# A hybrid convolution and gated-delta layer on one core: raw tokens in the first products, the fifth and sixth products tile by tile, the last product in pieces

## The chip, the cores and the metric

The kernel runs on one core of a Trainium2 chip. The metric is the device time of one execution in microseconds (us); lower is better. Before the change the median of three runs is 1960.46 us (1956.25 to 1960.53).

## The reference, cut to what matters

1024 tokens of width 1024, all in float32. Three residual stages, each behind an RMS norm:

```python
h = h + 0.5 * swiglu_ffn(rmsnorm(h, ffn1_norm), w1_in, w1_out)     # 1024 -> 2*2816 -> 1024
u = rmsnorm(h, mix_norm) @ w_mix_in                                # gates, convolution, q, k, v
h = h + concat([short_conv(u), gated_delta(u)]) @ w_mix_out
h = h + 0.5 * swiglu_ffn(rmsnorm(h, ffn2_norm), w2_in, w2_out)
return rmsnorm(h, final_norm)
# rmsnorm(x, w) = x * rsqrt(mean(x*x) + 1e-6) * w
```

## The kernel before, in words

The tokens lie transposed: eight tiles (d = 0 to 7) of 128 features by 512 tokens for each half of the tokens, `h[0]` and `h[1]`. Every float32 operand of a large product is split into a rounded part `hi` (ScalarE, L102) and the rest `lo` (VectorE, L103), and a product of two tiles is three matmuls (`mm3`, L190 to L194: hi·hi, lo·hi, hi·lo). Weights come through SyncE's queue into eight `raw` tiles (L95) and are split into seven pairs `whi`, `wlo`.

The products are saved by a Winograd form of Strassen's scheme: a `Pair` (L321) takes two column tiles of the weights and needs seven products of four `mm3` each instead of eight. The token blocks are A11, A12 (the first half, split in `split1`), S1, nS2, S3, S4 and A22 (`Blocks.sums`, L294, in three parts); the weight blocks are B11, B21, B22 and the sums T1 to T4, which GpSimd makes (`pool_tt`, L110). The head of a pair is product 1 (A11·B11, copied out of PSUM as `p1`, L351) and product 2 (added into the same bank, then `first`, L435). The body is products 6 (nS2·T2), 5 (S1·T1), 7, 4 and 3 (L364 to L407). Product 7 is added into the bank of product 6, L389 reads it, and product 4 goes on in the same bank.

At the start (`first_heads`, L607) the heads of five pairs run before the bodies. SyncE's queue fetches eight tiles of tokens by rows (`xtok`) for the norm's sums, then four token tiles and four weight tiles in turn. ScalarE squares the rows, GpSimd takes the power (L219), TensorE spreads the factor over the partitions (`spread`, L239, into the bank `rb`), VectorE scales each token tile by gain and factor (`norm1`, L281), and only then can a tile be split and used. The second half of the tokens follows the same way (`norms[1]`), and its `spread` releases `sums(0)`. `all_pairs` (L409) writes out the bodies of pairs 0 and 1 in turn: both sixth products, `sums(1)`, both fifth, `sums(2)`, both seventh, and so on. The same function is used by the first feed-forward stage, by the projection to q, k, v and by the second feed-forward stage.

`ffn_out` (L496) is the product with the second weight matrix: seven products of eleven steps (k = 0 to 10), each step four `mm3` (d = 0 to 3), one bank for each d. After the fifth (S1·T1) `t1_done` squares the first half and calls `after(26, 4)` (in the second feed-forward stage `after(30, 4)`): 26 `mm3` later TensorE sums the squares (`reduce`, L221), four later it spreads the factor. The weight sum T4 of the last product (A22·T4) is made on GpSimd, in its queue behind the norm's power. At the very end `reduce`, `spread` and `scale_out` run for the second half of the tokens with 512 columns at once.

A planner (`run_tasks`, L119) writes the code out: each task has a load, a preparation and a run; preparations are written four tasks ahead of the runs, loads nine. Tile's scheduler then orders instructions on an engine by the program order, except where one is ready earlier by its own model; `keep_in_program_order` forbids that. An engine runs its queue in order.

Of the kernel before, what the change touches and what calls it, by code (L numbers as in the profile page):

```python
# [56 lines left out]
def tile_hybrid(  # L57
# [145 lines left out]
    class Norm:  # L203
# [25 lines left out]
        def by_tokens(self, src):  # L229

            tot = const.tile([P, 8], F32, name="tot", tag="tot", bufs=2)
            for i, tile_ in enumerate(src):
                nc.scalar.activation(out=tile_, in_=tile_, func=AF.Square, accum_out=tot[:, i:i + 1])
# [33 lines left out]
    class Blocks:  # L267
# [3 lines left out]
        def __init__(self, h, which):  # L271
            self.h, self.g = h, V_N[which]
            self.s4 = []
            self.b = {n: [None] * KH for n in ("A11", "A12", "S1", "nS2", "S3", "S4", "A22")}
# [11 lines left out]

        def begin2(self, k):

            h2 = self.h[1]
            nc.scalar.activation(out=h2[k], in_=h2[k], func=AF.Copy, scale=self.gain(k))  # L290
# [3 lines left out]
        def sums(self, part, rb):  # L294

            h, b = self.h, self.b
            if part == 0:
                for k in range(KH):
                    s1, s2 = h[1][k], h[0][k]
                    nc.vector.tensor_tensor(out=s1, in0=s1, in1=rb, op=ALU.mult)  # L300
                    nc.vector.tensor_tensor(out=s2, in0=s2, in1=s1, op=ALU.subtract)  # L301
                    b["nS2"][k] = split(s2, slot)
                for k in range(KH):
                    b["S1"][k] = split(h[1][k], slot)
            if part == 1:
                for k in range(KH):
                    a22, s2 = h[1][k + KH], h[0][k]
# [13 lines left out]
    class Pair:  # L321
# [5 lines left out]
        def __init__(self, x, srcs, first, done):  # L327
            self.x, self.srcs, self.first, self.done = x, srcs, first, done
            self.r, self.t, self.w = {}, {}, {}
# [14 lines left out]
        def run_p1(self):  # L344
            self.x_ps = psum()
            prod(self.x_ps, self.w.pop("B11"), self.x.b["A11"], True)
            self.copy_p1()

        def copy_p1(self):
            self.p1 = temp4(F32, "p1")  # L350
            nc.scalar.copy(out=self.p1[:, 3:HALF + 3], in_=self.x_ps)  # L351

        def run_p2(self):
            prod(self.x_ps, self.w.pop("B21"), self.x.b["A12"], False)
            self.done("C11", self.first(self.x_ps))
# [5 lines left out]
        def head2(self):  # L361
            return self.run_p2, lambda: self.ready("B21"), lambda: self.get("B21")

# [45 lines left out]
    def all_pairs(pairs, x, norm2, between={}):  # L409
# [3 lines left out]
        for a in (0, 2):  # L413
            for n, two in enumerate(zip(*(p.body() for p in pairs[a:a + 2]))):
                if a == 0 and n in (1, 2):
                    task(None, lambda n=n: norm2.then(lambda: x.sums(n, norm2.rb)))
                for t in two:
                    task(*t)
# [11 lines left out]
    def gate_pair(x, w_in, j, gs, store):  # L430
        t = {}

        def first(ps):
            c = temp4(F32, "c11")
            nc.scalar.activation(out=c[:, 3:HALF + 3], in_=ps, func=AF.Silu)  # L435
# [18 lines left out]
    def ffn_in(x, norms, w_in, name, start=None):  # L454
# [31 lines left out]
        all_pairs(pairs, x, norms[1])  # L486
# [9 lines left out]
    def ffn_out(acc, fill, g_dr, w_out, t1_done, t2_done):  # L496
# [8 lines left out]
        def step(banks, a, b, k, start):  # L505
# [27 lines left out]
            def run():  # L533
                x, w = ops["x"], ops["w"]
# [934 lines left out]
```

## Time and profile before

| | |
|---|---|
| runs | 1956.25, 1960.46, 1960.53 us |
| profiled execution | 1959.77 us, of it 1958.0 us span |
| TensorE busy | 1833.8 us, 94% of the span |
| VectorE, ScalarE, GpSimd busy | 68%, 38%, 37% |
| mean granted TensorE clock | 0.971 |

A busy TensorE is not TensorE at its peak, since matmuls overlap in the records. In a stretch without waits 442 matmuls take 100 us. So a stretch is read by its count of matmuls against its length.

### The profile page before, as it was taken

What the parts mean: (1) busy time and instruction counts of PE and PEld (TensorE: products, weight loads), DVE (VectorE), ACT (ScalarE), POOL (GpSimd) and SP (SyncE); (2) the same over time, 40 slices, a digit from 0 to 9 for tenths busy, and PEclk for the clock granted to TensorE, in tenths of its full rate; (3) what the DMA queues carried; (4) which work ended last, traced back from release to release, by engine and by line L of the source; (5) the groups of instructions that cost most, each with busy time, mean ns of one, the idle gap of its engine ahead of it and who ended that gap; (6) DMA issues with size and microseconds to landing.
All of it is one profiled execution on the core that took longest, in us unless ns stands there. A gap on an engine that the chain in (4) does not pass through costs nothing.

```text
span 1958.0 us, 25016 instructions
## 1 busy us (share of the span) xinstructions
PE 1833.8 (94%) x8512; PEld 1493.6 (76%) x8512; DVE 1338.5 (68%) x1991; ACT 750.0 (38%) x1517; POOL 733.3 (37%) x510
## 2 busy tenths in 40 slices
PE   5799999999999899987799989998999999999996
PEld 4578888888888777676678877776888888888884
DVE  4876666567865797776974356688666566677655
ACT  6422323223544453377332243452323222344433
POOL 1464455355331434145311001036454355435142
PEclk9899999999999999998999979998999999999998
DMA  7144343437883423477742176423343434487532
GB/s 281 33 161 128 118 140 127 140 108 257 311 270 113 140 97 102 141 245 252 222 135 80 61 263 183 164 92 102 127 139 127 140 109 160 150 292 274 193 108 97
DMA packets 194512, 312.45 MB, mean 160 GB/s; under 512 B 27856, under 2 KB 48336, under 8 KB 194384
## 3 DMA queue, kind: packets, MB, share of 16 engines
q1 hardware_dynamic: 191216, 305.28, 47.0%
q10 hardware_dynamic: 3168, 5.57, 0.9%
q8 instruction: 67, 1.10, 0.2%
q14 instruction: 61, 0.50, 0.1%
HBM read 228.44 MB, written 82.33 MB: 159 GB/s over the span
## 4 chain that ended last, share of the span: by engine, by line
PE 74%; DVE 13%; issue 4%; DMA 3%; POOL 3%; ACT 3%; SPq 0%; POOLq 0%; DVEq 0%; ACTq 0%
PE ps_ps L192 20%; PE ps_ps L191 20%; PE ps_ps L193 20%; PE ps_mm L191 3%; PE ps_mm L192 3%; PE ps_mm L193 3%; DVE wlo L103 3%; PE ps_aux L862 1%; DVE lo L103 1%; DVE xb L1034 1%; DVE sv L1030 1%; DVE cv L774 1%; POOL T L110 1%; DMA raw<-w_in 1%; DVE h L301 1%
## 5 line engine op out<-in xcount | busy, mean ns | idle before, releaser
L191 PE MATMUL ps_ps<-hi,whi 128*128 128x512 f32 x1400 | 554.1, 396 | 23.0 <-DVE c L389 11.4
L193 PE MATMUL ps_ps<-hi,wlo 128*128 128x512 f32 x1400 | 552.7, 395 | 13.0 <-DVE wlo L103 12.9
L192 PE MATMUL ps_ps<-lo,whi 128*128 128x512 f32 x1400 | 553.0, 395 | 5.3 <-DVE lo L103 5.2
L103 DVE TENSOR_TENSOR wlo<-raw,whi 128x512 fp32r<-128x512 f32 x280 | 267.3, 964 | 119.4 <-ACT whi L102 118.4
L103 DVE TENSOR_TENSOR wlo<-T,whi 128x512 fp32r<-128x512 f32 x244 | 235.3, 978 | 144.5 <-ACT whi L102 142.4
L191 PEld LDWEIGHTS ps_ps<-hi,whi 128*128 128x128 f32 x1400 | 266.8, 191 | 85.4 <-issue 12.3
L193 PEld LDWEIGHTS ps_ps<-hi,wlo 128*128 128x128 f32 x1400 | 267.3, 191 | 71.7 <-DVE wlo L103 16.0
L192 PEld LDWEIGHTS ps_ps<-lo,whi 128*128 128x128 f32 x1400 | 266.9, 191 | 63.1 <-DVE lo L103 8.0
L110 POOL TENSOR_TENSOR T<-raw 128x512 f32<-128x512 f32 x144 | 224.6, 1561 | 232.3 <-DMA raw<-w_out 91.5
L191 PE MATMUL ps_ps<-ghi,whi 128*128 128x512 f32 x616 | 241.8, 393 | 7.2 <-ACT whi L102 7.2
L192 PE MATMUL ps_ps<-glo,whi 128*128 128x512 f32 x616 | 241.9, 393 | 1.4 <-DVE glo L103 1.4
L193 PE MATMUL ps_ps<-ghi,wlo 128*128 128x512 f32 x616 | 241.7, 393 | 1.2 <-DVE wlo L103 1.2
L102 ACT CAST whi<-raw 128x512 fp32r<-128x512 f32 x280 | 170.2, 617 | 86.1 <-PE ps_mm L192 19.1
L102 ACT CAST whi<-T 128x512 fp32r<-128x512 f32 x244 | 146.4, 617 | 81.4 <-POOL T L110 44.8
L191 PE MATMUL ps_mm<-hi,whi 128*128 128x512 f32 x384 | 158.0, 412 | 0.9 <-DVE u L400 0.9
L192 PE MATMUL ps_mm<-lo,whi 128*128 128x512 f32 x384 | 155.2, 404 | 1.2 <-DVE lo L103 1.2
L193 PE MATMUL ps_mm<-hi,wlo 128*128 128x512 f32 x384 | 154.2, 402 | 1.4 <-DVE wlo L103 1.4
L103 DVE TENSOR_TENSOR glo<-raw,ghi 128x512 fp32r<-128x512 f32 x154 | 128.9, 838 | 38.8 <-ACT ghi L102 37.2
L191 PEld LDWEIGHTS ps_ps<-ghi,whi 128*128 128x128 f32 x616 | 116.3, 189 | 33.6 <-ACT whi L102 8.4
L193 PEld LDWEIGHTS ps_ps<-ghi,wlo 128*128 128x128 f32 x616 | 116.3, 189 | 28.0 <-DVE wlo L103 2.7
L192 PEld LDWEIGHTS ps_ps<-glo,whi 128*128 128x128 f32 x616 | 116.4, 189 | 27.3 <-DVE glo L103 2.1
L110 POOL TENSOR_TENSOR T<-raw,T 128x512 f32<-128x512 f32 x50 | 73.3, 1465 | 167.2 <-DMA raw<-w_in 129.3
(226 smaller groups left out, 2286.5 us busy)
## 6 DMA issues: line engine op xcount, KB each, us to landing
raw<-w_in SPq DMA_DIRECT2D x264, 256.0 KB, 4.6
raw<-w_out SPq DMA_DIRECT2D x154, 256.0 KB, 4.3
raw<-w_qkv SPq DMA_DIRECT2D x36, 256.0 KB, 3.4
f1S<-S SPq DMA_DIRECT2D x33, 256.0 KB, 5.0
raw<-f1A SPq DMA_DIRECT2D x33, 256.0 KB, 3.9
raw<-f1S SPq DMA_DIRECT2D x33, 256.0 KB, 3.7
f2S<-S SPq DMA_DIRECT2D x33, 256.0 KB, 5.0
raw<-f2A SPq DMA_DIRECT2D x33, 256.0 KB, 4.5
```

The source lines that it names most:

```text
L102: tc.keep_in_program_order(nc.scalar.copy(out=hi, in_=src))
L103: nc.vector.tensor_tensor(out=lo, in0=src, in1=hi.bitcast(F32), op=ALU.subtract)
L110: tc.keep_in_program_order(nc.gpsimd.tensor_tensor(out=out, in0=in0, in1=in1, op=op))
L191: nc.tensor.matmul(out=ps, lhsT=whi, rhs=xhi, start=start, stop=False, skip_group_check=True)
L192: nc.tensor.matmul(out=ps, lhsT=whi, rhs=xlo, start=False, stop=False, skip_group_check=True)
L193: nc.tensor.matmul(out=ps, lhsT=wlo, rhs=xhi, start=False, stop=stop, skip_group_check=True)
L301: nc.vector.tensor_tensor(out=s2, in0=s2, in1=s1, op=ALU.subtract)
L774: nc.vector.scalar_tensor_tensor(out=acc, in0=u[:, i:i + HALF], scalar=vcol(wc + i), in1=acc, op0=ALU.mult, op1=ALU.add)
L862: nc.tensor.matmul(out=ps[:, sl], lhsT=lhs[:, sl], rhs=rhs[:, sl], start=start, stop=stop)
L1030: nc.vector.tensor_tensor(out=tv, in0=lrow[:, lo:hi].unsqueeze(2).broadcast_to([nb, n, j + 1]), in1=xrow[:, 0:j + 1].unsqueeze(1).broadcas ...
L1034: nc.vector.tensor_tensor(out=xv, in0=xv, in1=tv, op=ALU.subtract)
```

## The change

- Start: the first token tiles are fetched ahead of the rows. `split_raw` splits gain times token, without the norm's factor, and the first and second products of the five early pairs run on that. The factor (`rbs`) is put in by VectorE on leaving PSUM, in `copy_p1` and in `first`. The fifth pair's weights and all five B21 are fetched ahead of the second half's rows. `norm1` of the eight tiles still runs for the sums, and A11 and A12 are split once more, from the normed tokens, for the pairs from the sixth on (one tile every three `mm3`, after the bodies of pairs 0 and 1). One token tile lies in a `raw` tile.
- `sums(0)` splits S1 and nS2 block by block. `all_pairs` prepares T1 and T2 of pairs 0 and 1 first, then runs `both(k)`: for one block k the fifth and sixth products of both pairs; then `sums(1)`, the seventh products, `sums(2)`, and the rest. This holds for all three users of `all_pairs`.
- `after(26, 4)` and `after(30, 4)` become `after(14, 4)`.
- The small weights `wba` are loaded and split in a task after the first `ffn_out`, no longer wherever the scheduler puts them.
- Last product of the second `ffn_out`: steps k = 0 to 6 as before; steps 7 to 10 are held and run for one d after the other, with the add behind each. The closing norm's sum, power, spread, scaling and stores go in two halves of 256 columns. The ScalarE queue stores d = 1, 4 and 7.

```diff
+        def split_raw(self, d):
+            src = self.h[0][d]
+            hi, lo = slot(F32R, "hi"), slot(F32R, "lo")
+            tc.keep_in_program_order(nc.scalar.activation(out=hi, in_=src, func=AF.Copy, scale=self.gain(d)))
+            nc.vector.scalar_tensor_tensor(out=lo, in0=src, scalar=self.gain(d), in1=hi.bitcast(F32),
+                                           op0=ALU.mult, op1=ALU.subtract)
...
                 for k in range(KH):
-                    s1, s2 = h[1][k], h[0][k]
+                    s1 = h[1][k]
+                    s2 = self.s2[k] = slot(F32, "s2") if self.raw else h[0][k]
                     nc.vector.tensor_tensor(out=s1, in0=s1, in1=rb, op=ALU.mult)
-                    nc.vector.tensor_tensor(out=s2, in0=s2, in1=s1, op=ALU.subtract)
+                    nc.vector.tensor_tensor(out=s2, in0=h[0][k], in1=s1, op=ALU.subtract)
+                    b["S1"][k] = split(s1, slot)
                     b["nS2"][k] = split(s2, slot)
-                for k in range(KH):
-                    b["S1"][k] = split(h[1][k], slot)
...
         def copy_p1(self):
             self.p1 = temp4(F32, "p1")
-            nc.scalar.copy(out=self.p1[:, 3:HALF + 3], in_=self.x_ps)
+            if self.factor is not None:
+                nc.vector.tensor_tensor(out=self.p1[:, 3:HALF + 3], in0=self.x_ps, in1=self.factor, op=ALU.mult)
+            else:
+                nc.scalar.copy(out=self.p1[:, 3:HALF + 3], in_=self.x_ps)
...
+        def both(self, k):
+            if k == 0:
+                self.z, self.y = psum(), psum()
+            ks = slice(k * P, (k + 1) * P)
+            for ps, t, s in ((self.z, "T1", "S1"), (self.y, "T2", "nS2")):
+                w = self.w[t]
+                mm3(ps, w[0][:, ks], w[1][:, ks], *self.x.b[s][k], k == 0, k == KH - 1)
...
+                for one, two in zip(*products[:2]):
+                    task(None, one[1], one[2])
+                    task(None, two[1])
+                for k in range(KH):
+                    task(lambda k=k: [p.both(k) for p in pairs[:2]])
...
+            task(*head(early[4], 0))
+            task(lambda: [norms[0].spread(), scaled(), then()], lambda: [x.split_raw(d) for d in range(KH, KT)])
+            task(*head(early[0], 1))
+            task(*head(early[1], 1))
+            task(*head(early[2], 1))
+            task(*head(early[3], 1))
+            task(norms[1].spread)
+            task(*head(early[4], 1))
...
+                      {0: lambda: [later(3 * d, lambda d=d: x.split1(d)) for d in range(KT)]})
...
-            nm[0].after(26, 4)
+            nm[0].after(14, 4)
...
-            task(add)
+            if not by_tile:
+                task(add)
+                return
+            for d in range(KH):
+                task(lambda d=d: [one(d, i == KH - 1) for i, one in enumerate(held)] and add([d]))
...
+        for i in range(2):
+            two = slice(2 * i, 2 * i + 2)
+            for b in range(2 * i, 2 * i + 2):
+                nc.tensor.matmul(out=sums[:, b:b + 1], lhsT=last[1].acc[:, b * P:(b + 1) * P], rhs=ones[:, 0:1],
+                                 start=True, stop=True)
+            nc.vector.tensor_scalar(out=ms[:, two], in0=sums[:, two], scalar1=1.0 / D, scalar2=EPS,
+                                    op0=ALU.mult, op1=ALU.add)
+            nc.gpsimd.tensor_tensor(out=rs[:, two], in0=ms[:, two], in1=pneg[:, two], op=ALU.pow)
+        for i in range(2):
+            for b in range(2 * i, 2 * i + 2):
+                nc.tensor.matmul(out=last[1].rb[:, b * P:(b + 1) * P], lhsT=rs[:, b:b + 1].broadcast_to([P, P]),
+                                 rhs=ident, start=True, stop=True)
+            scale_out(1, slice(2 * i * P, (2 * i + 2) * P))
```

## Rows read from the trace of the kernel before

**Rows 1.** The page's head: span and TensorE's busy time.
```profile
span 1958.0 us, 25016 instructions
```

**Rows 2.** Busy time by stretches: stretch, its length, then busy us and (count) of TensorE matmuls, weight loads, VectorE, ScalarE, GpSimd, then granted clock, DMA share, GB/s.
```profile
0.00:25.00 25.00, 8.23 (x24) 6.25 (x25) 11.21 (x22) 14.28 (x33) 1.20 (x5) 1.00 0.94 337
25.00:50.00 25.00, 20.73 (x82) 16.17 (x81) 12.48 (x17) 16.00 (x35) 8.25 (x5) 0.86 0.59 213
50.00:75.00 25.00, 17.67 (x71) 13.40 (x70) 24.05 (x36) 13.77 (x25) 10.01 (x6) 0.87 0.05 13
100.00:116.50 16.50, 16.50 (x75) 13.67 (x74) 14.35 (x14) 3.89 (x7) 14.68 (x10) 1.00 0.56 191
200.00:300.00 100.00, 100.00 (x442) 82.85 (x442) 64.56 (x73) 29.05 (x54) 51.02 (x34) 1.00 0.40 132
649.20:686.00 36.80, 31.77 (x133) 24.33 (x133) 29.95 (x38) 17.65 (x31) 15.25 (x10) 1.00 0.48 158
715.00:745.00 30.00, 23.31 (x90) 17.80 (x89) 28.01 (x39) 14.31 (x29) 13.50 (x9) 0.93 0.11 35
1313.00:1345.00 32.00, 25.36 (x90) 19.33 (x89) 27.64 (x35) 12.51 (x23) 14.05 (x8) 0.84 0.13 42
1900.00:1937.30 37.30, 32.59 (x134) 25.93 (x133) 25.71 (x31) 13.92 (x25) 15.08 (x10) 0.95 0.38 127
```

**Rows 3.** Timeline of TensorE, start of the kernel: start, length, engine, line, operation, and in brackets the idle time before with what ended it.
```profile
20.07 0.80 PE L192 MATMUL ps_ps<-lo,whi 128*128 128x512 f32 x1 [1.72 <-DVE lo L103]
...
57.23 0.61 PE L191 MATMUL ps_ps<-hi,whi 128*128 128x512 f32 x2
...
71.25 0.80 PE L193 MATMUL ps_ps<-hi,wlo 128*128 128x512 f32 x1 [6.18 <-DVE wlo L103]
...
87.79 0.47 PE L191 MATMUL ps_ps<-hi,whi 128*128 128x512 f32 x1 [2.89 <-DVE c L389]
```

**Rows 4.** Timeline of the start on ScalarE (ACT) and VectorE (DVE).
```profile
3.96 0.63 ACT L233 ACTIVATE xtok<-xtok 128x512 f32<-128x512 f32 x1 [0.74 <-DMA xtok<-xtok]
11.86 0.62 ACT L102 CAST whi<-raw 128x512 fp32r<-128x512 f32 x1 [0.64 <-DMA raw<-w_in]
15.94 0.62 ACT L102 CAST whi<-raw 128x512 fp32r<-128x512 f32 x1 [0.75 <-DMA raw<-w_in]
22.67 0.27 ACT L696 CAST wba<-wba 128x96 fp32r<-128x96 f32 x1 [3.21 <-DVE wba L694]
...
51.27 0.69 DVE L300 TENSOR_TENSOR h<-h,ps_ps 128x512 f32<-128x512 f32 x1 [0.95 <-PE ps_ps L243]
...
71.72 0.68 DVE L103 TENSOR_TENSOR wlo<-T,whi 128x512 fp32r<-128x512 f32 x1
```

**Rows 5.** Groups of instructions over the whole span: line, engine, operation, output and inputs, shapes, count, then busy us and mean ns of one, then idle before.
```profile
L103 DVE TENSOR_TENSOR lo<-h,hi 128x512 fp32r<-128x512 f32 x76 | 60.4, 811 | 1.2 <-ACT hi L102 1.2
L389 DVE TENSOR_TENSOR c<-ps_ps,p 128x512 f32<-128x512 f32 x50 | 34.0, 681 | 11.4 <-PE ps_ps L193 11.1
L281 DVE SCALAR_TENSOR_TENSOR h<-h,vs,ps_ps 128x512 f32<-128x512 f32 x16 | 11.6, 742 | 5.3 <-PE ps_ps L243 3.6 <-DMA h<-xT 1.7
L301 DVE TENSOR_TENSOR h<-h 128x512 f32<-128x512 f32 x8 | 8.6, 1090 | 0.0
```

**Rows 6.** Timeline of GpSimd (POOL) and TensorE around the norms inside the two `ffn_out` (`nacc`: the sums of squares; `rs`: the power; `nT`: the weight sum T4).
```profile
618.70 5.77 POOL L211 TENSOR_TENSOR nacc<-nacc,sq 128x512 f32<-128x512 f32 x4 [2.67 <-ACT sq L209]
638.16 1.02 POOL L219 TENSOR_TENSOR rs<-ms,cs 128x4 f32<-128x4 f32 x1 [13.68 <-DVE ms L217]
...
1869.51 5.83 POOL L211 TENSOR_TENSOR nacc<-nacc,sq 128x512 f32<-128x512 f32 x4 [2.67 <-ACT sq L209]
1891.71 1.02 POOL L219 TENSOR_TENSOR rs<-ms,cs 128x4 f32<-128x4 f32 x1 [16.38 <-DVE ms L217]
...
1917.19 0.50 PE L191 MATMUL ps_ps<-ghi,whi 128*128 128x512 f32 x1 [4.06 <-ACT whi L102]
```

**Rows 7.** Timeline of TensorE and VectorE where the bodies of pairs 0 and 1 run in the q, k, v projection (first two rows) and in the second feed-forward stage.
```profile
730.76 0.50 PE L191 MATMUL ps_ps<-hi,whi 128*128 128x512 f32 x1 [1.14 <-ACT whi L102]
743.16 0.47 PE L191 MATMUL ps_ps<-hi,whi 128*128 128x512 f32 x1 [2.54 <-DVE c L389]
...
1320.03 0.68 DVE L103 TENSOR_TENSOR wlo<-T,whi 128x512 fp32r<-128x512 f32 x1
1326.00 0.50 PE L191 MATMUL ps_ps<-hi,whi 128*128 128x512 f32 x1 [1.16 <-ACT whi L102]
1340.07 0.47 PE L191 MATMUL ps_ps<-hi,whi 128*128 128x512 f32 x1 [3.15 <-DVE c L389]
```

**Rows 8.** Timeline of the end, all engines (ACTq: the DMA queue of ScalarE).
```profile
1938.94 0.39 PE L193 MATMUL ps_ps<-ghi,wlo 128*128 128x512 f32 x1
...
1940.49 2.28 DVE L211 TENSOR_TENSOR nacc<-nacc,sq 128x512 f32<-128x512 f32 x3
1942.83 1.87 PE L225 MATMUL ps_ps<-cs,nacc 128*128 128x1 f32 x8 [3.49 <-DVE nacc L211]
1946.04 2.08 PE L243 MATMUL ps_ps<-cs,rs 128*128 128x128 f32 x8 [1.35 <-POOL rs L219]
1948.78 3.38 DVE L1387 SCALAR_TENSOR_TENSOR h<-h,vs,ps_ps 128x512 f32<-128x512 f32 x5 [3.88 <-ACT rbs L1380]
1950.12 3.98 ACTq L1389 DMA_DIRECT2D out_dram<-h  x4
```

More of the change, by code (lines that the diff above doesn't have):

```diff
@@ L431, in gate_pair, with first @@
         t = {}
-        def first(ps):
+        def first(ps, factor):
             c = temp4(F32, "c11")
+            if factor is not None:
+                nc.vector.tensor_tensor(out=c[:, 3:HALF + 3], in0=ps, in1=factor, op=ALU.mult)
+                ps = c[:, 3:HALF + 3]
             nc.scalar.activation(out=c[:, 3:HALF + 3], in_=ps, func=AF.Silu)
@@ L485, in ffn_in @@
             start(pairs)
[L486 removed]
+        all_pairs(pairs, x, norms[1], between)
         return g_dr
@@ L503, in get, with step @@
             return load(w_out[2 * k + row][:, c * HALF:(c + 1) * HALF])
-        def step(banks, a, b, k, start):
+        def step(banks, a, b, k, start, held=None):
             r, ops = {}, {}
@@ L613, in first_heads @@
                 early[k].get("B11")
+            rows1 = by_tokens(0)
             get_x(0, *range(KH, KT))
-            norms[0].by_tokens(rows1)
-            norms[0].spread()
             for p in four:
                 p.x_ps = psum()
-                p.ready("B11")
-            def first(k):
-                x.norm1(norms[0].rb, k)
-                x.split1(k)
+            for p in early:
+                p.late_p1 = True
+            for k in range(KH):
+                x.split_raw(k)
+                four[k].ready("B11")
+            norms[0].by_tokens(rows1)
             def run(k):
@@ L1393, in out_t1, with out_t2 @@
                 last[0].square(d)
-            last[0].after(30, 4)
-            last[0].then(lambda: scale_out(0))
-        ffn_out(acc, fill, g_dr, w2_out, out_t1, lambda d: last[1].square(d, nc.vector))
-        run_tasks()
-        last[1].reduce()
-        last[1].spread()
-        scale_out(1)
+            last[0].after(14, 4)
+            last[0].then(lambda: [gain(0, d) for d in range(KT) if pre_scaled(d)] and scale_out(0))
+        def out_t2(d):
+            last[1].square(d, nc.vector)
+            if pre_scaled(d):
+                gain(1, d)
+        ffn_out(acc, fill, g_dr, w2_out, out_t1, out_t2, by_tile=True)
+        run_tasks()
+        last[1].rb = psum()
+        sums = psum()
+        ms, rs = (const.tile([P, 4], F32, name=n) for n in ("last_ms", "last_rs"))
+        for i in range(2):
[11 more added lines that the diff above has]
+            scale_out(1, slice(2 * i * P, (2 * i + 2) * P))
         while queue:
```

143 lines of the change are left out of this document (85 added, 58 removed).

## The prediction

> **What bounds the kernel now.** I read the table of stretches first. Between 200 and 300 us 442 matmuls fill the 100 us, 0.226 us each, and TensorE is the bound [rows 2]. Every stretch is then held against its count: its length less 0.226 us for each matmul is what TensorE lost there. Three kinds of place lose time, and the change touches all of them. One is the start: the first 75 us hold 177 records of matmuls, 40 us of work. The second is the stretch in which the bodies of pairs 0 and 1 run in the two later stages: 90 matmuls in 30.0 us (715 to 745) and in 32.0 us (1313 to 1345), against 20.3 us each, so 9.7 and 11.7 us are lost. The third is the last product of both `ffn_out`: 133 matmuls in 36.8 us and 134 in 37.3 us, so 6.7 and 7.0 us [rows 2]. To these comes the end, from the last matmul at 1939.2 to 1958.0 [rows 1, 8]: 18.8 us in which TensorE does next to nothing. Next I read, in the timelines, who ends each wait.
>
> **The start.** Before, steady matmuls begin at 20.07, and the bodies follow the fifth second product at 57.23 [rows 3]. The norm's rows came first over SyncE's queue; the four weight tiles that followed, each with a token tile, were cast from 11.86 to 15.94, 1.36 us a pair [rows 4]. So a tile lands each 0.68 us, and the eighth tile some 1.4 us before 11.86. With tokens and weights at the head of the queue the last of the four weights is therefore split at about 10.5 + 0.6 + 0.8 = 12 us. (ScalarE takes its first landed tile at 3.96 [rows 4], so it keeps up.) The 36 matmuls of blocks 1 to 3 then take 8 us at 0.226, or 12 us at the 0.34 that the 24 records of the first 25 us took (8.23 us) [rows 2]; I take 12, since this is a start too, and come to 24. Fifth first product 2.7 us (12 matmuls), `spread` 1.1, `rbs` and the first `p1` 1.4 (two VectorE steps of 0.68 [rows 5]; TensorE waits for this, since product 2 adds into the same bank), four second products 10.9, `spread` 1.1, fifth second product 2.7: the heads end near 44 instead of 57.2, and the second half's factor is spread near 41 instead of 51.
>
> The norm of the first half hides behind this: its eight rows now land at 11 to 16 us, ScalarE squares them by 18, the power is there at about 19.5, and the spread comes at 27. Moved behind it in SyncE's queue: the second four token tiles, six weight tiles (the B21 wait for `raw` tiles, seven now instead of eight, since a token tile holds one; four are free by 12 us), then the second rows and tokens, done by some 35 us. Also gone is a wait of ScalarE for `wba`, 3.21 us just ahead of the fifth pair's weights [rows 4].
>
> But then VectorE decides. From 51.27 on, where `sums(0)` begins [rows 4], it is full: 24.05 of the 25 us from 50 to 75 [rows 2], and the waits at 71.25 and 87.79 end on it [rows 3]. From 20 us the changed kernel asks of it, ahead of `sums(0)`: ten splits at 0.81 (8.1), nine factor steps at 0.68 (6.1), eight `norm1` at 0.74 (5.9) and four steps of `begin2`, which like L301 read two SBUF tiles, at 1.0 to 1.09 (4.2) [rows 5]: 24 us, so `sums(0)` starts at 44 and not 51.3. That is 7.3 us, less 1.4 for the two late factor steps; plus up to 6.5 us, since T3 is no longer behind the eight splits of `sums(2)` and the fifth and sixth products go block by block beside `sums(0)`. I take 9 us. Bounds: 4 (VectorE also pays part of what TensorE waits for at 44), and 17 (13 for the heads, and some of the wait at 71.25).
>
> Splitting A11 and A12 again is eight VectorE splits, 6.5 us, in the 16.5 us after the bodies of pairs 0 and 1, where VectorE is busy 14.35 [rows 2]: 4.3 us too much. Preparations are four tasks ahead (four times 2.7 us), and hide most of it; I take 1.5 us lost, bounds 0 and 4.3. A split beside GpSimd can cost more: L301, two inputs from SBUF, takes 1,090 ns, while L389, with one input from PSUM, takes 681 [rows 5]. The Trainium skill (GPSIMD Engine Reference, 8. Key points) says that GpSimd shares its SBUF interfaces with VectorE and contends with VectorE instructions of two SBUF inputs; the rows agree in sign, and by that rule the new factor steps, which read PSUM, stay cheap, while the second splits would cost 8.7 us, not 6.5.
>
> **The early norms in both `ffn_out`.** The power `rs` began at 638.16 and 1891.71 [rows 6], behind 26 and 30 `mm3` (0.68 us each) and 1.2 us of sum and mean. So the fifth product ended near 619.3 and 1870.1, and the new `reduce` stands 14 `mm3` or 9.5 us behind that, at 628.8 and 1879.6. The sums of squares end at 624.5 and 1875.3 [rows 6]: no new wait, with 4 us to spare. GpSimd, which sat idle 13.68 and 16.38 us for the mean with the T4 sums queued behind it, is free 8.1 and 10.9 us earlier. With T4 of the first steps done early, VectorE and ScalarE no longer hold up the adds of the sixth product, nor TensorE as at 1917.19 (4.06 us for a weight) [rows 6]. Of 6.7 us I take 5.5 (bounds 3 and 6.7), since in the first stage four sums of squares still stand in GpSimd's queue; of 7.0 I take 6 (bounds 4 and 7).
>
> **Bodies in the two later stages.** VectorE is busy 28.0 of 30 and 27.6 of 32 us [rows 2], so TensorE's waits go only as far as the order of VectorE's work matters. T3 now comes ahead of the eight splits of `sums(2)`: the wait for its weight (1.14 us at 730.76) and what follows can go. The wait at 743.16 and 1340.07 (2.54 and 3.15 us) ends on L389 [rows 7], which stands in VectorE's queue among the same splits; I leave most of it. 4 us each; bounds 0 and 8. Behind a wait of `both(0)` stands all of TensorE's queue; the banks it needs (four) come free with the first three second products.
>
> **The end.** Now from the last matmul: adds, squares and sums 3.6 us to 1942.8, `reduce` 1.9, mean and power 1.3, spread 2.1, copy 0.6, scaling 3.4, stores to 1958.0 [rows 8]. New: one add, one square, one sum (2.2), half a `reduce` (1.0), mean and power 1.3, half a spread 1.1, half a copy 0.4: the first scaling starts 6 us after the last matmul (before 9.6). VectorE then has twice five steps of 256 columns, about 0.4 each: 4 us, while the second power and spread run beside it. GpSimd's twice three end at 10.1 as well. Before, scaling ended 13 us behind the last matmul and the stores 5.8 later; now 10 and some 4.3: 14.3, a gain of 4.5. Bounds 2 (sixteen stores cost more to issue than eight) and 7.
>
> **Sum.** -9 + 1.5 - 5.5 - 4 - 4 - 6 - 4.5 = -31.5 us. The profiled execution took 1959.77 us (1958.0 of it the span), 0.7 below the median; I keep its base: 1928 us. All bounds against the change give 1951, all for it 1906.
>
> **Rivals.** *VectorE stays the bound.* What the start wins is eaten by the factor steps and the second splits, and both later stages keep their waits. For it: 24.05 of 25 us. Against it: its idle time in the first 50 us (26 us) [rows 2], in which much of the work now fits. Only 5.5, 6 and 4.5 are left: 1944.
>
> *TensorE gets all it can.* The start is worth 17, the bodies 8 each, the products 6.5 each, the end 5, the second splits 1.5: 1910. Against it: VectorE's load above.
>
> *Slower.* `both(0)` can't begin until all four weight sums are split, where the sixth products began with one. If VectorE's order stays, the last split ends at 72.4 [rows 4], 15 us after 57.2; at 1320.7 [rows 7] with the bodies ready near 1313.9 (48 matmuls, 10.9 us, ahead of the wait of 1.16 that ended at 1326.0 [rows 7]), 7 us; about as much in the middle stage. Less the 6.2 us of wait at 71.25 that this replaces, it costs 7 to 9 a place, 23 us; with 6.1 us of factor steps and 6.5 of splits paid in full, 35, against 16 from the norms and the end: 1979. It decides from some 5 us of added wait a place without the start's gain. Against it: the four sums are prepared with nothing but the second products' weights ahead of them.
>
> *The early norm does nothing*, since the last products wait for loads and not for GpSimd: 11.5 us are missing, 1940.
>
> **How the numbers follow.** Forecast 50% (1915 to 1941), VectorE 24%, all of it 13%, slower 7%, no gain from the norms 6%. From 1908 to 1947 some 2 in 10 are left out. A measurement of this kernel can tell 0.3%, 6 us, from no change: faster 0.91 (all cases but the slower one and the edge of VectorE's), same 0.03, slower 0.06.
>
> **What would show it.** Steady matmuls from 12 us; the second spread near 41; first fifth-product matmul at 45 to 49, the first fourth product near 79 instead of 87.8; `rs` in the two `ffn_out` at 630 and 1881 less what was won before; the last products in 31 to 32 us; 14 us from the last matmul to the end. I am wrong if sums are split later than the heads end, or if VectorE has no idle time up to 80 us and TensorE waits on it as before.

## The result and the profile after

| | before | after |
|---|---|---|
| median of eight runs, us | 1958.33 (1952.78 to 1964.81) | 1939.57 (1935.97 to 1949.1) |
| profiled execution, us | 1959.77 | 1937.25 |
| ratio after to before, 95% interval | | 0.991 (0.9887 to 0.9934) |

The change makes the kernel 0.9% faster, 18.8 us by the medians and 22.5 by the profiled executions (that of the changed kernel is 2.3 below its median, that of before 1.4 above). The forecast was 1928, 31.5 us less. The sign and the range hold; of the 31.5 us, 9 are missing by the profiled executions and 12.7 by the medians. The page's head and busy times of the changed kernel:

```profile
span 1935.5 us, 25088 instructions
...
PE 1831.5 (95%) x8512; PEld 1489.7 (77%) x8512; DVE 1345.2 (69%) x2016; ACT 754.2 (39%) x1521; POOL 742.9 (38%) x514
```

Both traces hold 8512 records of matmuls in nearly the same order. So the n-th record of one can be laid beside the n-th of the other, and the difference of their starts says how far ahead the changed kernel is at that point of the work. (Where the order differs, inside a stage, only the ends of the stage compare.) The steps of that difference say where time was won or lost:

| stretch, by record | after less before, us | change within it | forecast |
|---|---|---|---|
| start, to 300 | -8.8 | -8.8 | -9 |
| second split of A11, A12, 300 to 450 | -0.3 | +8.5 | +1.5 |
| 450 to 2500 | -0.2 | +0.1 | |
| last product of the first `ffn_out`, 2500 to 2750 | -5.2 | -5.1 | -5.5 |
| bodies in q, k, v, 2900 to 3100 | -4.6 | 0.0 | -4 |
| mixer, 3100 to 5750 | -9.5 | -4.9 | |
| bodies in the second feed-forward, 5750 to 5950 | -14.0 | -4.5 | -4 |
| 5950 to 8400 | -12.6 | +1.4 | |
| last product of the second `ffn_out`, 8400 to 8450 | -19.5 | -6.9 | -6 |
| end, to the span's end | -22.5 | -3.0 | -4.5 |

The rows leave out 2750 to 2900, where 0.6 us were lost. Inside the second row the lead is gone, at +0.9, by the 380th record (9.7 us lost), and 1.2 us come back by the 450th.

The table of stretches after the change answers [rows 2] (columns as there). The four stretches of 30 us begin earlier by what had been won.

```profile
0.00:25.00 25.00, 17.17 (x68) 12.86 (x68) 11.26 (x20) 18.29 (x39) 1.21 (x5) 1.00 0.96 343
25.00:50.00 25.00, 19.23 (x75) 14.71 (x76) 23.76 (x39) 14.92 (x32) 8.52 (x7) 0.90 0.57 207
50.00:75.00 25.00, 21.66 (x66) 14.11 (x65) 25.00 (x31) 13.09 (x24) 12.37 (x9) 0.76 0.13 42
100.00:110.00 10.00, 8.35 (x36) 6.28 (x34) 10.00 (x8) 2.41 (x5) 9.64 (x6) 1.00 0.71 231
110.00:120.00 10.00, 4.89 (x12) 3.86 (x13) 7.54 (x11) 1.14 (x2) 1.60 (x1) 0.67 0.01 2
...
644.20:675.50 31.30, 30.57 (x132) 24.26 (x131) 28.19 (x36) 16.98 (x31) 14.99 (x10) 1.00 0.58 181
709.00:740.00 31.00, 24.36 (x93) 19.46 (x94) 26.96 (x38) 14.41 (x29) 16.93 (x11) 0.89 0.16 51
1294.00:1324.00 30.00, 26.79 (x107) 21.65 (x106) 27.53 (x39) 17.59 (x31) 14.54 (x8) 0.89 0.19 61
1889.00:1919.80 30.80, 30.79 (x135) 24.97 (x133) 22.61 (x32) 13.76 (x24) 8.53 (x6) 1.00 0.19 61
```

The first 25 us hold 68 matmuls instead of 24. But VectorE is now busy all of the 25 us from 50 on, and from 110 to 120 TensorE does 12 matmuls, where 44 fit. Both last products fill their stretch (132 in 31.3 us, 135 in 30.8; before 36.8 and 37.3). The waits of TensorE behind this, from its timeline, beside [rows 3, 7]:

```profile
6.70 0.80 PE L191 MATMUL ps_ps<-hi,whi 128*128 128x512 f32 x1 [6.70 <-ACT whi L102]
27.40 0.47 PE L191 MATMUL ps_ps<-hi,whi 128*128 128x512 f32 x1 [3.53 <-DVE p L365]
...
78.18 0.77 PE L191 MATMUL ps_ps<-hi,whi 128*128 128x512 f32 x1 [4.43 <-DVE c L418]
...
115.11 0.76 PE L191 MATMUL ps_ps<-hi,whi 128*128 128x512 f32 x1 [6.16 <-DVE c L418]
...
731.85 0.76 PE L191 MATMUL ps_ps<-hi,whi 128*128 128x512 f32 x1 [5.99 <-DVE u L391]
...
1298.98 0.80 PE L193 MATMUL ps_ps<-hi,wlo 128*128 128x512 f32 x1 [3.21 <-DVE wlo L103]
```

The first is the wait for the first cast; the others end on VectorE. Behind each of these the granted clock stands at 0.50 for some us, the lower of TensorE's two levels (28 to 31, 79 to 81, 116 to 120, 732 to 736 and 1300 to 1304 us), and a matmul starts every 0.43 us instead of every 0.23. So such a wait costs more than its own length: the 12 matmuls from 115.11 on take 5.2 us, 2.5 more than at the pace of 200 to 300 us, and with the 6.16 of the wait that is 8.6 us. What VectorE did ahead of the wait at 115.11 (its timeline; the second splits are the rows `lo<-h,hi`):

```profile
96.61 1.77 DVE L103 TENSOR_TENSOR lo<-h,hi 128x512 fp32r<-128x512 f32 x1
98.31 0.68 DVE L409 TENSOR_TENSOR u<-ps_ps,p 128x512 f32<-128x512 f32 x1
98.91 1.19 DVE L103 TENSOR_TENSOR lo<-h,hi 128x512 fp32r<-128x512 f32 x1
...
101.73 1.78 DVE L103 TENSOR_TENSOR lo<-h,hi 128x512 fp32r<-128x512 f32 x1
...
105.73 2.86 DVE L103 TENSOR_TENSOR lo<-h,hi 128x512 fp32r<-128x512 f32 x2
108.52 1.75 DVE L103 TENSOR_TENSOR wlo<-T,whi 128x512 fp32r<-128x512 f32 x1
...
114.28 0.68 DVE L418 TENSOR_TENSOR c<-ps_ps,p 128x512 f32<-128x512 f32 x1
```

L418 is the add that frees the bank for the next product. It stands behind all eight splits. With three more of 0.68 us between 110 and 114 the eight took 9.64 us, 1.2 each. GpSimd was busy 9.64 of the 10 us up to 110, and idle when the last two of 0.68 us ran (from 112.0 on); the steps that read PSUM kept 0.68 throughout.

One part of the change did not happen as written: the small weights `wba` were still split at the start. Their load is issued at 29.8 us, and VectorE's step, which took 0.19 us in the kernel before, takes 1.18 us among the factor steps:

```profile
40.35 1.18 DVE L764 TENSOR_TENSOR wba<-wba 128x32 f32<-128x32 f32 x1
```

The norms inside `ffn_out` (GpSimd's timeline, beside [rows 6]): the power comes 8.3 and 23.2 us earlier, of which 0.2 and some 13 us had been won before, and T4 follows at once.

```profile
629.86 1.02 POOL L219 TENSOR_TENSOR rs<-ms,cs 128x4 f32<-128x4 f32 x1 [5.52 <-DVE ms L217]
630.85 3.77 POOL L110 TENSOR_TENSOR nT<-nT,raw 128x512 f32<-128x512 f32 x3
...
1868.53 1.02 POOL L219 TENSOR_TENSOR rs<-ms,cs 128x4 f32<-128x4 f32 x1 [5.52 <-DVE ms L217]
```

The end, all engines, beside [rows 8]:

```profile
1921.22 0.69 DVE L211 TENSOR_TENSOR nacc<-nacc,sq 128x512 f32<-128x512 f32 x1 [0.69 <-ACT sq L209]
...
1923.74 1.20 PE L1495 MATMUL ps_ps<-cs,last_rs 128*128 128x128 f32 x4
...
1925.38 2.05 DVE L1464 SCALAR_TENSOR_TENSOR h<-h,vs,ps_ps 128x256 f32<-128x256 f32 x5 [1.31 <-ACT rbs L1458]
1925.89 6.11 SPq L1466 DMA_DIRECT2D out_dram<-h  x10
...
1927.57 1.19 PE L1495 MATMUL ps_ps<-cs,last_rs 128*128 128x128 f32 x4 [2.64 <-POOL h L1462]
...
1929.21 2.05 DVE L1464 SCALAR_TENSOR_TENSOR h<-h,vs,ps_ps 128x256 f32<-128x256 f32 x5 [1.78 <-ACT rbs L1458]
```

The second half's spread waits 2.64 us for the readers of the first half, which lies in the same bank. The scaling ends 11.6 us behind the last large matmul (forecast 10), the kernel 4.3 us behind that, as forecast.

### The profile page after: what moved, and what is told of

Same layout as the page of the kernel before. It is cut to its first block, busy times and chain, and to the rows that moved or that the text cites. A ratio compares the mean times of both kernels' runs of the same rounds, so it can differ in the third digit from the quotient of the medians.

```text
span 1935.5 us, 25088 instructions
## 1 busy us (share of the span) xinstructions
PE 1831.5 (95%) x8512; PEld 1489.7 (77%) x8512; DVE 1345.2 (69%) x2016; ACT 754.2 (39%) x1521; POOL 742.9 (38%) x514
## 4 chain that ended last, share of the span: by engine, by line
PE 77%; DVE 13%; DMA 4%; issue 3%; ACT 2%; POOL 1%; SPq 0%; ACTq 0%; POOLq 0%; DVEq 0%
PE ps_ps L191 21%; PE ps_ps L193 21%; PE ps_ps L192 21%; PE ps_mm L191 3%; PE ps_mm L192 3%; PE ps_mm L193 3%; DVE wlo L103 3%; DVE lo L103 2%; PE ps_aux L933 1%; DVE cv L845 1%; DVE xb L1105 1%; DVE sv L1101 1%; DMA raw<-w_in 1%; DMA kT<-qkv_dr 1%; PE ps_aux L975 1%
## 5 line engine op out<-in xcount | busy, mean ns | idle before, releaser
L103 DVE TENSOR_TENSOR wlo<-raw,whi 128x512 fp32r<-128x512 f32 x280 | 255.3, 921 | 117.0 <-ACT whi L102 115.9
L110 POOL TENSOR_TENSOR T<-raw 128x512 f32<-128x512 f32 x144 | 231.6, 1608 | 223.2 <-DMA raw<-w_out 83.2
L110 POOL TENSOR_TENSOR T<-raw,T 128x512 f32<-128x512 f32 x50 | 78.0, 1559 | 162.2 <-DMA raw<-w_in 112.7
```

The source lines that it names most:

```text
L103: nc.vector.tensor_tensor(out=lo, in0=src, in1=hi.bitcast(F32), op=ALU.subtract)
L110: tc.keep_in_program_order(nc.gpsimd.tensor_tensor(out=out, in0=in0, in1=in1, op=op))
```

## The experiments

All edits are on the changed kernel. "Ahead" compares starts of the same matmul record in the profiled executions. But for the last two, each kernel ran once, and the eight runs of the changed kernel alone lie 13 us apart. So a single time settles little; what is won or lost is read from the records of a stretch. An edit can shift line numbers by a few: L392 and L419 in two of the kernels are L391 and L418 of the changed one.

**How far two executions differ.** No edit.

> The changed kernel once more, with no edit: how far two executions of the same program differ stage by stage, since the mixer (3100th to 5700th matmul) showed differences of up to 5 us where nothing was changed. Theory: within 0.5 us everywhere in the feed-forward stages, up to 5 us in the mixer. Rival (the programs differ there in what the scheduler ordered): within 0.5 us in the mixer too.

1937.3 us. But for the first matmuls (0.4 us) the two executions agree within 0.3 us up to the 435th record. There one wait of 0.98 us more puts them 0.8 apart, up to the 3000th. In the mixer they drift up to 3.7 us apart (near the 3512th record) and come back; outside 3300 to 3700 they agree from the 3050th on within 0.5 us, but for 0.8 near the 3954th. So neither theory holds in full: inside the mixer two executions of one program do differ, but over the whole of it only by 0.4 us. Both executions are near the fastest of the eight; what the slower ones lose, and where, no trace shows.

**No second split.** All pairs run products 1 and 2 on the raw tokens; the factor is kept in a constant tile.

```diff
-                rbs = slot(F32, "rbs")
+                rbs = rb2
                 nc.vector.tensor_copy(out=rbs, in_=norms[0].rb)
+                for p in pairs:
+                    p.factor = rbs
                 for p in early:
-                    p.factor = rbs
                     p.copy_p1()
...
-                      {0: lambda: [later(3 * d, lambda d=d: x.split1(d)) for d in range(KT)]})
+                      {})
```

> A11 and A12 are not split a second time. All 22 pairs of the first feed-forward run products 1 and 2 on the raw tokens, and all take the factor on leaving PSUM (VectorE instead of ScalarE copies p1; two VectorE steps of 0.68 us more for each of the 17 later pairs, in a stage where VectorE is a third idle). Read by the start of the same matmul record in this kernel and in the changed one. Theory A (the eight second splits, up to 1.77 us each beside GpSimd, stand in VectorE's queue ahead of the factor-free adds of products 7 and 4, and took back the 8.8 us that the start had won): the wait of 6.16 us at 115.11 us is gone or below 2, and from the 345th matmul on this kernel runs 7 to 10 us ahead of the changed one, so about 1929 us. Rival B (the bodies of pairs 0 and 1 are short of VectorE whatever is queued, or the raw tile that a token tile holds is what is missing: it stays held here until the third part of the sums): the wait stays over 4 us, and no more than 3 us are won. Rival C (the 34 steps more are not hidden): 7 to 10 us ahead at the 345th matmul, and up to 23 us lost again by the 2500th.

1935.24 us. The wait at 115 is gone and the kernel is 7.0 us ahead at the 345th record: between 320 and 345 it wins 8.6, as theory A had it. By the 450th it is 0.3 ahead, by the 2500th 2.6 behind. TensorE's timeline shows the new wait, on VectorE's copy of p1, behind which product 2 has to wait:

```profile
137.11 0.76 PE L191 MATMUL ps_ps<-hi,whi 128*128 128x512 f32 x1 [3.76 <-DVE p L365]
```

**The same, p1 copied by ScalarE.** The pairs of the start (`late_p1`) keep VectorE's copy.

```diff
+            nc.scalar.copy(out=p1, in_=self.x_ps)
             if self.factor is not None:
...
+                nc.vector.tensor_tensor(out=p1, in0=p1, in1=self.factor, op=ALU.mult)
```

> As the kernel without second splits, but ScalarE copies p1 of the 17 later pairs out of PSUM, as in the changed kernel, and VectorE multiplies the copy by the factor in place behind it. In the kernel without second splits 7.0 us were won by the 345th matmul and gone by the 450th, in a wait of 3.76 us at 137.11 that ended on VectorE's copy of p1, and what the slow clock added. Theory A2 (TensorE then stood behind VectorE's queue only because that copy frees the bank that product 2 adds into): 6 to 9 us ahead of the changed kernel at the 345th matmul and still 5 to 9 ahead at the 450th and the 2500th, so 1930 to 1934 us. Rival (with the start earlier, the weights of the pairs from the fifth on come no earlier, since their loads stand behind stores in SyncE's queue, which was still from 108 to 118 us): a wait of the same size near 130 to 137 that ends on a load or on a weight's split, and no more than 1 us won at the 450th.

1931.68 us. Again 8.6 us are won between records 320 and 345. It is 5.0 ahead at the 345th, 3.3 at the 450th (a wait of 1.61 us remains), 2.3 at the 2500th; from the 300th to the 450th it wins 7.8. It is less than theory A2 said, because this kernel and the one before it reach the 320th record 3.6 and 1.6 us late: the scheduler had put the copy of the factor ahead of the A12 splits on VectorE, where it stood idle for 3.55 us.

**Splits spread out.** `later(6 * d)` for `later(3 * d)`.

> The second splits one tile every six matmul triples (4 us) instead of every three (2 us). Theory A (VectorE's queue): 8 splits then ask 1.8 of every 4 us instead of 1.8 of every 2, so the loss of some 9 us between the 320th and the 345th matmul falls to 0 to 4 us, and the kernel comes to 1931 to 1936 us. Rival B (the missing raw tile, held until the eighth split, or GpSimd's sums of that stretch): held longer or as long, so the loss stays at 7 us or more, perhaps a little later, and the time at 1936 to 1942.

1938.41 us. The wait falls to 3.26 us and 2.6 us are won from record 320 to 345, but by the 450th 1.8 of it are lost again: of the 8.5 us 7.7 stay. That is the rival's number, and it left the raw tile open as a cause. TensorE's and VectorE's timelines show where it went:

```profile
113.03 0.77 PE L191 MATMUL ps_ps<-hi,whi 128*128 128x512 f32 x1 [3.26 <-DVE c L418]
137.35 0.47 PE L191 MATMUL ps_ps<-hi,whi 128*128 128x512 f32 x1 [2.33 <-DVE u L409]
```
```profile
129.74 1.79 DVE L103 TENSOR_TENSOR lo<-h,hi 128x512 fp32r<-128x512 f32 x1
...
134.85 1.75 DVE L103 TENSOR_TENSOR lo<-h,hi 128x512 fp32r<-128x512 f32 x1
136.52 0.68 DVE L409 TENSOR_TENSOR u<-ps_ps,p 128x512 f32<-128x512 f32 x1
```

Two splits moved into the next stretch in which VectorE is full, and cost their 1.8 us there.

**One split, the raw tile held.** Beside the edits of "The same, p1 copied by ScalarE":

```diff
+                      {0: lambda: later(24, lambda: nc.scalar.copy(out=temp(F32, "hold"), in_=h[0][KT - 1]))})
```

> As the kernel with one split whose p1 ScalarE copies, but the raw tile in which the eighth token tile lies stays held as long as in the changed kernel: ScalarE reads it once more, 24 matmul triples behind the bodies of pairs 0 and 1 (the copy goes nowhere). VectorE's queue is as without second splits. Spreading the second splits had left the loss as large, only later, so both causes were still open. Theory A (VectorE's queue): 8 to 9 us are won between the 320th and the 345th matmul, as without the hold (8.6). Rival (loads wait for the eighth raw tile): the wait of 4 to 6 us near 115 us is back, and under 4 us are won there.

1931.47 us; 8.8 us won from record 320 to 345, and 8.2 from 300 to 450. Counted in matmuls the tile is held as long, though not in time: its last read stands at 106.88, the eighth second split of the changed kernel at 113.68. The wait of 6.16 us, which ended on an add that reads no weight, is gone here. So the raw tile is not what TensorE waited for.

**The late norm again.** `after(26, 4)` and `after(30, 4)`.

> The sum of squares in both second halves of the feed-forward stands 26 and 30 triples behind the fifth product again, as in the kernel before; all else as changed. Theory: the early sum is what won 5.0 us in the first and, with the tile-by-tile order not needed, 6.9 us in the second last product, since GpSimd no longer sits with T4 queued behind the power. Then 4 to 6 us are lost between the 2500th and the 2800th matmul and 5 to 7 between the 8400th and the 8450th: 1946 to 1951 us. Rival (the tile-by-tile order of steps 7 to 10 won the second): 4 to 6 in the first, under 2 in the second. Rival (the early sum does nothing): under 1.5 in both.

1949.32 us: 5.2 us lost between records 2500 and 2750, 7.5 between 8400 and 8450. The power starts 1883.60 behind 16.22 us of idle GpSimd, and TensorE waits as before:

```profile
667.67 0.64 PE L191 MATMUL ps_ps<-ghi,whi 128*128 128x512 f32 x1 [2.14 <-ACT whi L102]
1910.14 0.80 PE L191 MATMUL ps_ps<-ghi,whi 128*128 128x512 f32 x1 [5.16 <-ACT whi L102]
```

Steps 7 to 10 ran tile by tile here too, and gained nothing without the early norm.

**Bodies in the old order.**

```diff
-                for k in range(KH):
-                    task(lambda k=k: [p.both(k) for p in pairs[:2]])
...
+                if a == 0 and n in (1, 2):
+                    task(None, lambda n=n: norm2.then(lambda: x.sums(n, norm2.rb)))
```

> The bodies of pairs 0 and 1 in the order of the kernel before (both sixth products, second part of the sums, both fifth, third part, both seventh ...), in all three stages that use them; sums(0) block by block, the raw start and all else as changed. Theory: the block order is worth 8.6 us in the second feed-forward (5750th to 5900th matmul), nothing in the q, k, v stage (where the third part's splits now stand ahead of the sixth product's add: 6 us of wait that ate what T3 in front had won), and some 3 us at the start, since the bodies can begin with the first two blocks. So 11 us slower than the changed kernel, 1948 us. Rival (the 8.6 us come from elsewhere in the stage, such as the order of sums(0)): under 3 us in the second feed-forward, 1937 to 1942 in all.

1939.63 us, not 1948. The start loses 2.8 us by the 450th record, as expected, and the second feed-forward 4.8 (records 5750 to 5950); in q, k, v only 1.2 are won (2900 to 3100): three waits of 0.74, 2.25 and 2.48 us stand there in place of the one of 5.99. The 8.6 expected for the second feed-forward was misread: it counted from the 5800th record, inside the stage, at which the changed kernel had already lost 4.1 us of its lead.

**S4 behind A22.**

```diff
+                if a == 0 and n == 3:
+                    task(None, lambda: norm2.then(lambda: x.sums(3, norm2.rb)))
```

> The third part of the sums in two: the four splits of A22 where they are, the four of S4 behind the preparations of the fourth products (only the third products need them). Theory (order in VectorE's queue): the adds of L391 and L418 come up to four splits earlier; the waits at 78.18 (4.43 us) and 731.85 (5.99 us) fall by 2 to 4 us each, and the q, k, v stage wins 2 to 6 us with the slow clock it no longer meets; the second feed-forward is as it was. Rival (VectorE is simply full there, whatever stands first): the same waits a little later, under 1 us won in each.

1940.6 us. The wait in q, k, v stays (6.00 us), the one at 78 grows to 7.78. But the order was hardly tested. In q, k, v one S4 split stood ahead of L391, and now a weight split of the same 0.68 us stands there, still behind the four A22 splits (5.73 us). At the start the first two S4 splits, 3.42 us at 76.44, still stand ahead of the add that frees the bank, and two weight splits besides. So the gain that was expected did not come, and the theory stays open.

**Two banks, and sums(0) paced.**

```diff
-        norm2.then(lambda: x.sums(0, norm2.rb))
+        if x.raw:
+            norm2.then(lambda: x.sums(0, norm2.rb))
+        else:
+            norm2.then(lambda: [later(4 * k, lambda k=k: x.sums(0, norm2.rb, k)) for k in range(KH)])
...
-        last[1].rb = psum()
+        closing = [psum(), psum()]
```

> Two edits at places that do not touch. (1) The two halves of the closing spread go into two PSUM banks. Theory: the second half's spread waited 2.64 us at 1927.57 only because the first half's readers used the same bank; it now starts behind the first half's, within 0.5 us of its power, and the stretch from the last large matmul to the end is 1.5 to 2.6 us shorter. Rival (VectorE's ten scaling steps and the stores set the end): shorter by under 0.7 us. (2) In the q, k, v stage and the second feed-forward the four blocks of sums(0) are written four matmul triples apart instead of all at once. Theory: the weight split that TensorE waited for at 1298.98 (3.21 us, then the slow clock to 1303.8) no longer stands behind twelve steps of sums(0), and between the 5750th and the 5850th matmul 3 to 5.5 us are won. Rival (the work of VectorE is the same and the wait moves to the bodies): won there and lost again by the 5950th.

1932.49 us. Pacing wins 4.2 us in q, k, v (records 2900 to 3100) and 1.8 in the second feed-forward, where 4.7 are won by the 5800th record (the wait of 3.21 us falls to 1.52) and 3.0 lost again: the rival there. In q, k, v VectorE's timeline of the changed kernel, then GpSimd's, and then VectorE and TensorE of this one:

```profile
724.78 5.72 DVE L103 TENSOR_TENSOR lo<-h,hi 128x512 fp32r<-128x512 f32 x4
...
731.02 0.68 DVE L391 TENSOR_TENSOR u<-ps_ps,p 128x512 f32<-128x512 f32 x1
```
```profile
716.59 6.43 POOL L110 TENSOR_TENSOR T<-raw 128x512 f32<-128x512 f32 x1 [2.61 <-DVE wlo L103]
...
723.01 2.99 POOL L110 TENSOR_TENSOR T<-raw,T 128x512 f32<-128x512 f32 x2
```
```profile
723.83 2.49 DVE L103 TENSOR_TENSOR lo<-h,hi 128x512 fp32r<-128x512 f32 x4
```
```profile
727.66 0.47 PE L191 MATMUL ps_ps<-hi,whi 128*128 128x512 f32 x1 [1.46 <-DVE u L391]
```

The same four A22 splits, still ahead of L391, take 2.49 us instead of 5.72, and the wait falls from 5.99 to 1.46.

At the end the wait for the bank is gone, and the scaling of both halves takes 4.00 us in place of 5.9 from first to last. Counted from the last large matmul the end comes 0.3 us earlier, not 1.5: the rival. (The granted clock is 0.50 from 1918 on in this execution, and the first of the closing sums took 1.01 us instead of 0.65, so some 0.4 us more may be hidden.) The scaling now ends 10.1 us behind the last large matmul, and the kernel 5.5 behind the scaling, not 4.3. All engines, then the table of stretches:

```profile
1919.65 2.39 PE L1499 MATMUL ps_ps<-cs,last_rs 128*128 128x128 f32 x8
...
1921.29 4.00 DVE L1468 SCALAR_TENSOR_TENSOR h<-h,vs,ps_ps 128x256 f32<-128x256 f32 x10 [1.31 <-ACT rbs L1462]
...
1921.80 5.95 SPq L1470 DMA_DIRECT2D out_dram<-h  x10
```
```profile
1924.00:1926.00 2.00, 0.00 (x0) 0.00 (x0) 1.29 (x4) 0.00 (x0) 1.48 (x3) 0.50 1.04 341
1926.00:1928.00 2.00, 0.00 (x0) 0.00 (x0) 0.00 (x0) 0.00 (x0) 0.00 (x0) 0.50 1.05 341
```

**A22 and S4 split as they are run.**

```diff
-                    task(None, lambda: norm2.then(lambda: x.sums(1, norm2.rb)))
+                    task(lambda: x.sums(2, norm2.rb), lambda: norm2.then(lambda: x.sums(1, norm2.rb)))
...
-                    task(None, lambda: norm2.then(lambda: x.sums(2, norm2.rb)))
+                    task(lambda: x.sums(3, norm2.rb))
```

> The changed kernel with the third part of the sums written as it is run: the four splits of A22 behind the adds L391 of the sixth products, the four of S4 behind the adds of the seventh. Moving S4 alone had left the wait of 6 us in the q, k, v stage as it was; there the four A22 splits stand ahead of L391 and take 5.72 us beside GpSimd's sums. Theory (it is A22's place): the wait of 5.99 us at 731.85 is below 1.5 and the stage wins 3 to 6 us; the fourth products may wait up to 2 us for A22 instead. At the start, where L391 stood ahead of A22 already (waits 0.77 and 4.43 at 67.68 and 78.18), the first stays and the second falls by 1 to 3. Rival (VectorE's backlog, not its order): the wait only moves behind the seventh products, under 1 us won.

1947.7 us; it did not do what it was written for. Tile's scheduler still put three of the four A22 splits ahead of L391 on VectorE:

```profile
730.39 5.10 DVE L103 TENSOR_TENSOR lo<-h,hi 128x512 fp32r<-128x512 f32 x3
735.41 0.68 DVE L392 TENSOR_TENSOR u<-ps_ps,p 128x512 f32<-128x512 f32 x1
```

(L392 is L391 of the changed kernel.) The waits are 6.46 us in q, k, v and 9.29 at the start. Whether the order alone would help stays open.

**All that won.**

> All that won, together: one split of A11 and A12, with p1 copied by ScalarE and the factor put in behind it; the raw splits of A12 and the copy of the factor in written order on VectorE (in the kernels with one split the copy stood ahead of them, idle 3.55 us for the spread, and the heads came 2.3 to 4.5 us later); the blocks of sums(0) four triples apart in the two later stages; the closing spread in two banks; and the eight stores of the second half as whole tiles, four on each queue, behind the second cut. Theory: 8 us ahead of the changed kernel behind the start (5 without the written order), 4 in the q, k, v stage, 2 in the second feed-forward, 1 to 2 at the end, since SyncE's queue needed 5.95 us to issue ten stores and ended the kernel with two banks alone: 1922 to 1927 us, 1.6 to 1.9% ahead of the kernel before. Rival (gains of one stage are taken back in the next, as those of the start were): 1930 or more.

Median of five runs 1925.5 us (1922.49 to 1931.59), ratio to before 0.9843 (0.982 to 0.9866): faster than before, and its slowest run is below the fastest of the changed kernel (1935.97). The time lies where it was forecast, but not all its parts do. Against the changed kernel it is 9.6 us ahead at the 380th record and 4.6 at the 2500th, where 8 were forecast. The 34 steps more on VectorE go with that loss: between 200 and 300 us VectorE is busy 73.3 us instead of 63.6, and TensorE does 438 matmuls, not 443. Then come 4.2 us in q, k, v, 1.3 in the mixer, where nothing was forecast, 1.8 in the second feed-forward, and nothing at the end, where whole tiles took back what two banks had won. The stretches of its end:

```profile
1918.00:1920.00 2.00, 0.00 (x0) 0.00 (x0) 0.00 (x0) 0.00 (x0) 0.00 (x0) 0.50 1.03 376
1920.00:1922.00 2.00, 0.00 (x0) 0.00 (x0) 0.00 (x0) 0.00 (x0) 0.00 (x0) 0.50 1.03 382
```

**The same with A22 and S4 split as they are run.**

> The kernel with all that won, and A22 and S4 split as they are run. Theory (order): its waits of 1.42 and 1.68 us in each of the two later stages and of 4.41 us at 78.09 shrink, so 2 to 5 us less than its 1925.5: 1920 to 1924 us. Rival (with the blocks of sums(0) paced, nothing is left to win by order): within 1.5 us of 1925.5 us.

Median of six runs 1941.25 us, ratio 0.9904 (0.9885 to 0.9922): both theories miss. The waits are 9.23 us at 83.21, 6.55 in q, k, v and 6.54 in the second feed-forward. Here too three A22 splits (5.11 us at 1317.52) stand ahead of the add that frees the bank, so the order that the theory speaks of was not made.

## Why the prediction was right or wrong

- **Start**: right, 8.8 us of 9. The mechanism was the one named: products on raw tokens, with the norm behind them. The signs given for it came: the second spread at 40.01 (forecast 41), the first matmul of the bodies at 45.18 (45 to 49), the first fourth product at 78.18 (79). One sign of being wrong came too: VectorE is full from 50 to 75, and TensorE waits 4.43 us for it at 78.18. The lead is 12.9 us at the 100th record (13 was the bound for the heads), and 8.8 are left at the 300th.
- **Second split of A11 and A12**: this term failed. It was set at 1.5 us, at most 4.3, as preparing ahead would hide the rest; 8.5 were lost (9.6 in the second execution), nearly all that the start had won. Two kernels without it win 8.6 between records 320 and 345, one with the raw tile held 8.8; of the 8.5 from 300 to 450, 7.8 and 8.2 come back where ScalarE copies p1. The step that failed is the overlap: the splits were not hidden, but stood in VectorE's queue ahead of the add that TensorE waited for. The prediction priced a split at 0.81 us, the mean of all its uses, and took VectorE's load from the stretch before the change. Here the eight took 1.2 us each, those beside GpSimd up to 1.78, and the earlier start left no idle time in which to hide them (10.00 of 10 us busy). No run has all eight with GpSimd idle, so how much of the loss is their price and how much their place in the queue is not shown. The Trainium skill (GPSIMD Engine Reference, 8. Key points) says that GpSimd contends with VectorE instructions of two SBUF inputs; by that rule the prediction had 8.7 us for the eight. The trace agrees: 9.64, while steps that read PSUM stayed at 0.68.
- **First `ffn_out`, and the last product of the second**: right, 5.1 and 6.9 us of 5.5 and 6; the products' stretches are 31.3 and 30.8 us (forecast 31 to 32). Undoing the early norm alone gives 5.2 and 7.5 back, so the rival "the early norm does nothing" falls.
- **Bodies in q, k, v**: wrong, 0 of 4. The waits for T3's weight and on L389 are gone, as forecast; but the four A22 splits stand ahead of L391, and the wait of 5.99 us is new. With them at 2.49 us instead of 5.72, 4.2 us are won. The old order is better by 1.2 us here.
- **Bodies in the second feed-forward**: right in size, 4.5 of 4, and partly by luck, for it is the difference of two parts: 5.5 lost, which nothing in the forecast covers, as a head's weight stands behind `sums(0)` in VectorE's queue, then 10 won.
- **End**: 3.0 of 4.5; from the last large matmul to the end it is 15.9 us, not 14.3. The bank that both halves share was overlooked; with it the scaling ends at 11.6 us instead of 10. But it is not all that was missing: without it the scaling ends at 10.1, and the end comes only 0.3 us earlier. The forecast let the stores end 4.3 us behind the scaling. Sixteen stores are 2.1 MB; at 341 GB/s that is 6.2 us from when they flow, whatever VectorE does.
- **Mixer**: 4.9 us were won where nothing was forecast. This is luck, and it covers part of what the second split cost: without it the profiled gain would be 17.6 us. Two executions of one kernel differ by 0.4 us over the mixer; the other kernels, whose edits leave its code alone, differ from the changed one by -2.0 to +3.5. At the seam to the second feed-forward VectorE's order does differ, with fewer weight splits among the last adds, and TensorE's wait there is shorter (before, then after):

```profile
1282.01 0.47 PE L191 MATMUL ps_ps<-hi,whi 128*128 128x512 f32 x1 [2.38 <-DVE h L1330]
1274.15 0.47 PE L191 MATMUL ps_ps<-hi,whi 128*128 128x512 f32 x1 [1.50 <-DVE h L1401]
```

Up to there every engine works on tiles of the same names in the same order in both kernels. What won the rest stays open.

The rivals: by the number alone "The early norm does nothing" (1940) and "VectorE stays the bound" (1944) lie nearer to the median than the forecast. The first falls by the experiment. The second named the second splits, which ate the start's gain, and it holds in q, k, v, but not in the second feed-forward, where 4.5 us were won. "TensorE gets all it can" needed 17 us from the start. For "Slower", a wait of `both(0)` for four weight sums was not seen; its other half, the splits paid in full, is what happened.

## What to carry to other kernels

Work that is added off the critical path has the price of the stretch into which it falls after the change, not before it: an earlier start moves the full engine's backlog forward with it. Price it by the longest row of that kind, not by its mean, where GpSimd is busy. At the end of a kernel, divide the bytes to store by the rate that the trace shows before counting on faster arithmetic, and where the scheduler may reorder, look at the engine's queue before believing that a step written later runs later.

## What was not expected of the hardware

- One 128x512 addition on GpSimd took 6.43 us at 716.59, beside back-to-back VectorE steps with two SBUF inputs, which kept their 0.6 to 0.7 us each; in quieter stretches it takes 1.3 us (1.29 at 1893.49). So either engine can be the one that pays. (Spans on GpSimd are rough.)
- A wait of 6.16 us costs TensorE more than itself: in the 10 us around it the mean granted clock was 0.67 of full speed, a mean over its two levels of 1.2 and 2.4 GHz, with 12 matmuls done.
- Stores in pieces of 256 columns flowed at 341 GB/s, whole tiles at 376 to 382, and at 379 to 383 in the kernel before (1951 to 1955 us). So the cut that lets the scaling start earlier also slows the stores; with whole tiles behind the second cut the gain in rate was lost in starting later.
